# Mean squares with the squares as stationary operand, and GpSimd's first block sums held back behind the start

## The chip, the cores and the metric

The kernel runs on one core of one Trainium2 chip. The metric is the device time in microseconds of one execution; lower is better. TensorE multiplies, VectorE and ScalarE work on tiles, GpSimd does the same with its own program, and SyncE (SP) only issues transfers. Every engine runs its own instructions in the order in which they stand in its queue, and waits at an instruction until what it needs is done.

## The reference

One layer of a decoder trunk on 1024 rows of 1024 values, in float32. The part that the change touches, shortened:

```python
h = layer_norm(x, ln_in_g, ln_in_b)
proj = h @ w_in                       # 11,296 columns: 44 pairs of 256 and the dt columns
u, b_gate, c_gate, z_a, z_s, xbc, dt_raw, g_a, g_s = jnp.split(proj, ...)
y_a = (silu(z_a) * b_gate * conv3(c_gate * u)) @ w_a_out
y_s = ssd_chunked(...) + d_skip * xs  # scan over 8 chunks of 128 rows, 4 groups
hg = (y_s * silu(z_s)) in 4 groups of 512 channels
hg = hg * rsqrt(mean(square(hg)) + 1e-5)   # per row and group
y_s = (hg * norm_s_g) @ w_s_out
h = layer_norm(alpha * h + (sigmoid(g_a) * y_a + sigmoid(g_s) * y_s) @ w_o, ln_g, ln_b)
```

## The kernel before

**Start.** Eight tiles x0 to x7 of 128 rows are loaded by SP. `stats` and `factors` make mean and reciprocal deviation on VectorE with a root on ScalarE (L348), `norm` applies them (L362 on ScalarE, L360 on VectorE for x3 and x7). TensorE transposes the tiles by 128 x 128 blocks into eight PSUM banks: x0 to x3 at L397, x4 to x7 in `second_half` at L419. For each k, `evac` copies a bank to `hf` on ScalarE (L371), and VectorE makes from it a rounded high part (the cast L375) and a low part (`sub_split`, L106): `b11` and `b21` for the first half of the rows. Before that TensorE runs matmuls on a zeroed tile `warm` (L320).

**Products.** A pair is two weight tiles of 128 columns each. The pair's 256 columns times 1024 rows are computed as seven products of blocks (half of the depth by half of the rows) instead of eight (j = 1 to 7): 1 is a11 with b11, 2 is a12 with b21, 3 is s4 with b22, 4 is a22 with t4, 5 to 7 are s1 to s3 with t1 to t3. GpSimd makes s1, s2, s3 in `combine` (L239 to L245) and s4 in `combine_last` (L253); t1 to t4 come from `quarter_sums` on VectorE with copies by ScalarE (L434). Each weight block is split too: `whip` (high, ScalarE L279 or VectorE L281) and `wlop` (low, VectorE L106). A product is four times three matmuls with 512 moving columns: high by high (L979), high by low (L980), low by high (L981). The first three pairs (`EARLY` = 3) are computed while the second half of the rows is being normalised; their results go through `oa` (L995, L988). `dps` (L446, L447) is the projection for dt.

**Scan.** The 32 chunks (four groups of eight) run as small stages between the products of the other pairs. A chunk ends with squares on ScalarE, two folding additions on GpSimd (L705, L706) and `s_sum`: a matmul with one column of ones as the stationary operand and the folded squares as the moving one, the sum of 128 rows in one row of PSUM (L715), ScalarE's copy of that row (L717) and its store to the DRAM line `ssq_d` (L718). At the eighth chunk `group_rstd` reads the line back as 128 x 8 on GpSimd's queue (L724), takes the root (`rsqrt`: ScalarE L89, VectorE L90 to L97) and stores the factors to `rst_d` (L727) on the same queue. Later stages read them from there for the y products (L822 to L824).

**Order.** The list `items` sets the order of the products. For the early pairs it is products 1 and 2 of pair 0, of pair 1, of pair 2, then 3, 6, 5, 7, 4 of the three in turn. The scheduler merges this with the other work, and each engine keeps the order that results. SP issues the loads in program order: x0 to x3, the constants, the dt weights, the four blocks of pair 0, then the rest.

Of the kernel before, what the change touches and what calls it, by code (L numbers as in the profile page):

```python
# [19 lines left out]
F32 = mybir.dt.float32  # L20
F32R = mybir.dt.float32r
AF = mybir.ActivationFunctionType
ALU = mybir.AluOpType
PSUM = bass.MemoryType.PSUM

P = 128
L = 1024
D = 1024
KT = D // P
HALF = 512  # L30
NCH = 8
H = 32
G = 4
# [12 lines left out]
def trunk_kernel(ctx: ExitStack, tc: tile.TileContext, x, w_in, w_dt, w_a, w_s, w_o, par, con,  # L46
# [10 lines left out]
    bc_d = [tc.dram_tile([P, 2, L], F32, name=f"bc_d{g}") for g in range(G)]  # L57
    cum_d = tc.dram_tile([H, L], F32, name="cum_d")
    ecum_d = tc.dram_tile([H, L], F32, name="ecum_d")
    ssq_d = [tc.dram_tile([1, L], F32, name=f"ssq_d{g}") for g in range(G)]  # L60
    rst_d = [tc.dram_tile([1, L], F32, name=f"rst_d{g}") for g in range(G)]

    cst = ctx.enter_context(tc.tile_pool(name="cst", bufs=1))
# [21 lines left out]
    def rsqrt(pool, r, v, n, tag):  # L85

        ve = pool.tile([P, n], F32, tag=tag + "a", name=tag + "a")
        q = pool.tile([P, n], F32, tag=tag + "b", name=tag + "b")
        S.activation(q, v, AF.Sqrt, bias=eps_t, scale=1.0)  # L89
        V.tensor_scalar(ve, v, EPS, -0.5, ALU.add, ALU.mult)  # L90
        V.reciprocal(r, q)
        if n == 1:
            V.scalar_tensor_tensor(q, r, ve, r, ALU.mult, ALU.mult)
        else:
            V.tensor_tensor(q, r, r, ALU.mult)
            V.tensor_tensor(q, q, ve, ALU.mult)
        V.scalar_tensor_tensor(r, q, 1.5, r, ALU.add, ALU.mult)  # L97
# [7 lines left out]
    def sub_split(lo, full, hi, eng):  # L105
        return eng.tensor_tensor(lo, full, hi.bitcast(F32), ALU.subtract)  # L106
# [48 lines left out]
    def rawt(name):  # L155
        return ap.tile([P, HALF], F32, tag="raw", name=name, bufs=8)

    def bank(tag, name):
        return pa.tile([P, HALF], F32, tag=tag, name=name, bufs={"U": 2, "yy": 2}.get(tag, 1))
# [26 lines left out]
    EARLY = 3  # L186
# [6 lines left out]
    pairs += [gates[1], *conv_pairs[6], gates[2], gates[3], *conv_pairs[7], gates[4], gates[5], gates[6], gates[7]]  # L193
    NP = len(pairs)
    assert NP == 44
    items = [("p", p, j) for p in range(EARLY) for j in (1, 2)]
    items += [("p", p, j) for j in (3, 6, 5, 7, 4) for p in range(EARLY)]
    late = None
    for p in range(EARLY, NP):
        items += [("p", p, 1)] + ([late] if late else []) + [("p", p, j) for j in (2, 6, 5, 7, 4)]  # L200
# [9 lines left out]

    raws, s1s, ops = {}, {}, {}

    def fetch(n):

        if n >= len(items) or items[n][:2] in raws or items[n] in raws:
            return
        kind, i, j = items[n]
        if kind == "p":
            blocks = {}
            for w in ("a11", "a12", "a21", "a22"):  # L220
                k0 = (int(w[2]) - 1) * HALF
                r = est.tile([P, HALF], F32, name=f"e{i}_{w}") if i < 2 else rawt(f"raw{i}_{w}")
                SP.dma_start(r, w_in[pairs[i][int(w[1])], :, k0:k0 + HALF])
                blocks[w] = r
            raws[kind, i] = blocks
        else:
            r = rawt(f"raw_{kind}{i}_{j}")
            SP.dma_start(r, w_a[i, :, j * HALF:(j + 1) * HALF] if kind == "a" else
                         w_s[4 * i + j // 2, :, j % 2 * HALF:(j % 2 + 1) * HALF])
            raws[items[n]] = r  # L230

    def combine(p):

        if p in s1s:
            return
        r = raws["p", p]
        s1, s2 = (est.tile([P, HALF], F32, name=f"e{n}_{p}") if p < 2 and n == "s1" else
                  r["a11"] if p < 2 else ap.tile([P, HALF], F32, tag=n, name=f"{n}_{p}") for n in ("s1", "s2"))
        Gp.tensor_tensor(s1, r["a21"], r["a22"], ALU.add)  # L239
        if p < 2:  # L240
            Gp.tensor_tensor(r["a21"], r["a11"], r["a21"], ALU.subtract)
            Gp.tensor_tensor(s2, s1, r["a11"], ALU.subtract)
        else:
            Gp.tensor_tensor(s2, s1, r["a11"], ALU.subtract)
            Gp.tensor_tensor(r["a21"], r["a11"], r["a21"], ALU.subtract)  # L245
        s1s[p] = {"s1": s1, "s3": r["a21"], "s2": s2}
# [48 lines left out]


    xs = []
    for s in range(NCH):
        xt = full_unit(s, f"x{s}")
        SP.dma_start(xt, x[s * P:(s + 1) * P, :])  # L300
        xs.append(xt)
        if s == 3:
            SP.dma_start(con_t, con)
            SP.dma_start(par_t, par)
            wdt_raw = rawt("wdt_raw")[:, :KT * H].rearrange("p (k h) -> p k h", k=KT)
            SP.dma_start(wdt_raw, w_dt)
            fetch(0)

    db_t, al_t = (cdec_t.rearrange("p h c -> p (h c)")[:, i * H:(i + 1) * H] for i in range(2))
    SP.dma_start(db_t, dt_bias.partition_broadcast(P))  # L310
# [1 line left out]
    wdt = est.tile([P, KT, 2 * H], F32R, name="wdt")  # L312


    warm = rawt("warm")
    dT = [rawt("dT0"), rawt("dT1")]
    V.memset(warm, 0.0)
    wps = bank("c4", "warm")
    for i in range(7):
        PE.matmul(wps, lhsT=warm[:, :P], rhs=warm, start=True, stop=True)  # L320

    last = {}
# [1 line left out]
    def q(eng, f):  # L324

        if eng in last:
            with tc.issue_after(last[eng].ins):
                ins = f()
        else:
            ins = f()  # L330
        last[eng] = ins
        return ins
# [24 lines left out]
    def norm(s, eng):  # L357
# [3 lines left out]
        else:  # L361
            q(S, lambda: S.activation(xt, xt, AF.Identity, bias=nb, scale=r))  # L362


    hf = [{}, {}]

    def evac(hf_i, k, ps):
        if k % 4 not in hf[hf_i]:
            hf[hf_i][k % 4] = full_unit(8 + 2 * (k % 4) + hf_i, f"hf{hf_i}{k % 4}")
        full = hf[hf_i][k % 4][:, k // 4 * HALF:(k // 4 + 1) * HALF]  # L370
        q(S, lambda: S.activation(full, ps, AF.Identity, bias=pc(C_LB + k), scale=pc(C_LG + k)))  # L371
        name = {(0, 0): "b11", (0, 1): "b21", (1, 1): "b22"}.get((hf_i, k // 4))
        if name:
            u = b_unit(name, k % 4)
            q(V, lambda: V.tensor_copy(u[:, 0, :], full))  # L375
            q(V, lambda: sub_split(u[:, 1, :], full, u[:, 0, :], V))

    for s in (0, 1):
        stats(s, 0)
# [14 lines left out]
        last[V] = prep(0, V)  # L394
    for s in (0, 1, 3, 2):
        for k in range(KT):
            PE.transpose(trs[k][:, s % 4 * P:(s % 4 + 1) * P], xs[s][:, k * P:(k + 1) * P], ident)  # L397
    for k in range(KT):
        evac(0, k, trs[k])
        if k in (4, 6):  # L400
# [168 lines left out]
    later, now = {}, [0]  # L569
# [5 lines left out]
    def srows(g, c):  # L575
        return slice(c * P, (c + 1) * P)
# [131 lines left out]
    def s_store(n):  # L708
        g, c = divmod(n, NCH)
        SP.dma_start(gat_d[g][:, :, srows(g, c)], YT[n])  # L710

    def s_sum(n):
        g, c = divmod(n, NCH)
        ps = bank("tr", f"trs{n}")
        PE.matmul(ps[0:1, 256:384], lhsT=ones[:, 0:1], rhs=ZS[n][:, 0, :], start=True, stop=True)  # L715
        row = sd["p"].tile([1, P], F32, tag="row", name=f"row{n}", bufs=1)
        S.activation(row, ps[0:1, 256:384], AF.Copy, scale=1.0 / 512.0)  # L717
        S.dma_start(ssq_d[g][:, srows(g, c)], row)  # L718
        if c == NCH - 1:
            group_rstd(g)  # L720

    def group_rstd(g):
        ms = cst.tile([P, NCH], F32, tag="ms", name=f"ms{g}")
        Gp.dma_start(ms, ssq_d[g].squeeze(0).rearrange("(p c) -> p c", c=NCH))  # L724
        r = cst.tile([P, NCH], F32, tag="rr", name=f"rr{g}")
        rsqrt(cst, r, ms, NCH, "rq")
        Gp.dma_start(rst_d[g].squeeze(0).rearrange("(p c) -> p c", c=NCH), r)  # L727

    NS = G * NCH
    micro = []  # L730
# [492 lines left out]
```

## Time and profile before

| | |
|---|---|
| median of 3 runs | 1432.3 us (1431.84 to 1434.41) |
| profiled execution | 1434.14 us, its span 1432.2 us |
| TensorE | busy 1391.3 us, 97%, mean granted clock 0.991 |
| VectorE, ScalarE, GpSimd | busy 975.1, 708.8, 484.7 us |
| granted clock of TensorE in 20:25, 25:30, 30:35 us | 0.85, 0.50, 0.62; 1.00 in the slices from 35 to 80 |

The profile is one execution. Busy time counts the instructions of an engine; a wait is idle time of an engine, put down to what released it. A granted clock of 1.00 is 2.4 GHz, one of 0.50 is 1.2 GHz. Times in the rows are from the start of the span.

### The profile page before, as it was taken

The page shows a single profiled execution, that of the slowest core. Times are in us where ns is not written, and L with a number is a line of the kernel's source. Part 1 is how long each engine was busy: PE and PEld are TensorE (multiplying, and loading weights), DVE is VectorE, ACT ScalarE, POOL GpSimd, SP SyncE. Part 2 cuts the span into 40 slices and gives each one's busy share as a digit, 9 for nine tenths or more (in the row PEclk, how much of TensorE's full clock was granted, in tenths as well). Part 3 has the DMA queues.
Part 4 walks back from the last instruction along what each step waited for, and adds up shares of the span by engine and source line. Part 5 has one row for each costly group of instructions (what it writes and reads, how often), then busy time and mean ns, then how long its engine had stood idle before and what let it go on. Part 6 is the DMA issues. An engine that isn't in the chain of part 4 may idle for free. (4 is left out here: it accounts for less than half of the span.)

```text
span 1432.2 us, 18457 instructions
## 1 busy us (share of the span) xinstructions
PE 1391.3 (97%) x6522; PEld 1100.9 (77%) x6522; DVE 975.1 (68%) x1423; ACT 708.8 (49%) x1227; POOL 484.7 (34%) x374
## 2 busy tenths in 40 slices
PE   6999999999999999999999999999989999999997
PEld 3777877787877787877787777878768888888786
DVE  7967878877678867778877768585464463224774
ACT  3664556555557565566555665656452231113421
POOL 4012324444334534334535234444230000000496
PEclk8999999999999999999999999999999999999999
DMA  6022354545344555445554445454547764223322
GB/s 234 16 96 89 110 141 132 144 148 146 125 132 135 137 155 149 135 114 156 130 167 117 151 126 143 145 147 129 184 150 268 233 226 137 90 81 119 123 101 77
DMA packets 166717, 198.14 MB, mean 138 GB/s; under 512 B 10944, under 2 KB 116320, under 8 KB 166624
## 3 DMA queue, kind: packets, MB, share of 16 engines
q1 hardware_dynamic: 158096, 167.12, 39.7%
q10 hardware_dynamic: 8272, 29.81, 5.3%
q8 instruction: 51, 0.84, 0.2%
q14 instruction: 42, 0.34, 0.1%
q0 software_dynamic: 256, 0.03, 0.0%
HBM read 146.29 MB, written 50.63 MB: 137 GB/s over the span
## 5 line engine op out<-in xcount | busy, mean ns | idle before, releaser
L106 DVE TENSOR_TENSOR wlop<-raw_a,whip 128x512 fp32r<-128x512 f32 x210 | 183.1, 872 | 171.3 <-ACT whip L279 66.7
L979 PE MATMUL p<-b,whip 128*128 128x512 f32 x352 | 144.0, 410 | 3.6 <-ACT a L781 3.4
L979 PE MATMUL pU<-t,whip 128*128 128x512 f32 x352 | 144.7, 413 | 1.7 <-ACT oa L1014 1.7
L279 ACT ACTIVATE whip<-raw_a 128x512 fp32r<-128x512 f32 x210 | 127.6, 622 | 36.9 <-issue 10.5
L979 PE MATMUL p<-t,whip 128*128 128x512 f32 x352 | 141.8, 403 | 1.7 <-DVE oa L988 1.7
L980 PE MATMUL p<-b,whip 128*128 128x512 f32 x352 | 140.3, 399 | 0.0
L981 PE MATMUL p<-b,wlop 128*128 128x512 f32 x352 | 140.2, 398 | 0.0
L981 PE MATMUL pU<-t,wlop 128*128 128x512 f32 x352 | 139.1, 396 | 1.0 <-DVE wlop L106 0.9
L981 PE MATMUL p<-t,wlop 128*128 128x512 f32 x352 | 139.2, 395 | 0.4 <-DVE wlop L106 0.4
L980 PE MATMUL pU<-t,whip 128*128 128x512 f32 x352 | 139.0, 395 | 0.0
L980 PE MATMUL p<-t,whip 128*128 128x512 f32 x352 | 138.9, 395 | 0.0
L647 POOL TENSOR_TENSOR xw<-xd,dte_t 128x256 f32<-128x256 f32 x56 | 46.9, 838 | 258.7 <-DVE xd L633 258.7
L904 POOL TENSOR_TENSOR res<-res,ag 128x1024 f32<-128x1024 f32 x8 | 19.6, 2455 | 276.4 <-ACT res L903 271.6
L823 PE MATMUL p_ws<-y,whis 128*128 128x512 f32 x256 | 100.9, 394 | 0.0
L822 PE MATMUL p_ws<-y,whis 128*128 128x512 f32 x256 | 100.8, 394 | 0.0
L824 PE MATMUL p_ws<-y,wlos 128*128 128x512 f32 x256 | 100.7, 393 | 0.0
L106 DVE TENSOR_TENSOR wlos<-raw_s,whis 128x512 fp32r<-128x512 f32 x32 | 22.1, 692 | 113.0 <-PE p_ws L824 89.3
L239 POOL TENSOR_TENSOR s<-raw_a,raw_a 128x512 f32<-128x512 f32 x42 | 69.7, 1660 | 85.4 <-DVE wlop L106 81.7
L253 POOL TENSOR_TENSOR raw_a<-raw_a,s 128x512 f32<-128x512 f32 x42 | 66.0, 1571 | 95.5 <-issue 87.3
L979 PEld LDWEIGHTS p<-b,whip 128*128 128x128 f32 x352 | 66.9, 190 | 26.5 <-issue 4.3
L106 DVE TENSOR_TENSOR wlop<-s,whip 128x512 fp32r<-128x512 f32 x84 | 80.1, 966 | 9.4 <-PE p L981 6.3
L613 ACT ACTIVATE em<-em,cum_t 128x128 f32<-128x128 f32 x256 | 81.3, 389 | 7.3 <-ACT ob L557 4.4
(219 smaller groups left out, 3340.8 us busy)
## 6 DMA issues: line engine op xcount, KB each, us to landing
raw_a<-in_w_in_dram SPq DMA_DIRECT2D x168, 256.0 KB
em<-cum_d SPq DMA_DIRECT2D x64, 256.0 KB
xg_d<-cv ACTq DMA_DIRECT2D x16, 512.0 KB
xT<-xg_d SPq DMA_DIRECT2D x32, 256.0 KB
z<-zs_d SPq DMA_DIRECT2D x32, 256.0 KB
gat_d<-y SPq DMA_DIRECT2D x32, 256.0 KB
gt<-gat_d SPq DMA_DIRECT2D x16, 512.0 KB
raw_s<-in_w_s_dram SPq DMA_DIRECT2D x32, 256.0 KB
```

The lines of the kernel that those rows point to most:

```text
L106: return eng.tensor_tensor(lo, full, hi.bitcast(F32), ALU.subtract)
L239: Gp.tensor_tensor(s1, r["a21"], r["a22"], ALU.add)
L253: Gp.tensor_tensor(a12, a12, s1s[p]["s2"], ALU.subtract)
L279: S.activation(flat(hi), src, AF.Copy)
L613: S.activation(em[:, h, :], em[:, h, :], AF.Relu, bias=cum_t[:, 8 * g + 4 * i + h, c:c + 1], scale=-1.0)
L647: Gp.tensor_tensor(xw, XD[n, i], dte_t[:, hs, c].unsqueeze(2).to_broadcast([P, HG, HD]), ALU.mult)
L822: PE.matmul(ps, lhsT=hi[:, k, :], rhs=u[:, 0, :], start=start, stop=False)
L823: PE.matmul(ps, lhsT=hi[:, k, :], rhs=u[:, 1, :], start=False, stop=False)
L824: PE.matmul(ps, lhsT=lo[:, k, :], rhs=u[:, 0, :], start=False, stop=stop)
L979: PE.matmul(ps, lhsT=hi[:, k, :], rhs=u[:, 0, :], start=first, stop=False, skip_group_check=True)
L980: PE.matmul(ps, lhsT=hi[:, k, :], rhs=u[:, 1, :], start=False, stop=False, skip_group_check=True)
L981: PE.matmul(ps, lhsT=lo[:, k, :], rhs=u[:, 0, :], start=False, stop=(k == 3), skip_group_check=True)
```

## The change

- `warm` is zeroed by GpSimd, not VectorE, as its first work; six matmuls run on it instead of seven, and four more of 256 columns between the transposes of x1 and x3.
- SP's loads stand in another order: `a11` and `a12` of the three early pairs, the dt weights and x4 to x7 come ahead of all `a21` and `a22`. The dt weights go into the tile `dT0`.
- `items` has product 1 of the three early pairs, then product 2 of the three.
- In `combine`, the first sum of an early pair waits for `b_done[0]`, the last low split of `b21` (k = 3).
- `s_sum` has the folded squares as the stationary operand and the column of ones as the moving one. The sum of a chunk is a column of PSUM, which ScalarE copies into column c of the tile `MS[g]` in SBUF. `ssq_d`, the stores to it and the read are gone, `group_rstd` is merged into `s_sum`, and the store of the factors writes element (p, c) to position 128 c + p instead of 8 p + c.

```diff
@@ -57,7 +57,6 @@
     bc_d = [tc.dram_tile([P, 2, L], F32, name=f"bc_d{g}") for g in range(G)]
     cum_d = tc.dram_tile([H, L], F32, name="cum_d")
     ecum_d = tc.dram_tile([H, L], F32, name="ecum_d")
-    ssq_d = [tc.dram_tile([1, L], F32, name=f"ssq_d{g}") for g in range(G)]
     rst_d = [tc.dram_tile([1, L], F32, name=f"rst_d{g}") for g in range(G)]
 
     cst = ctx.enter_context(tc.tile_pool(name="cst", bufs=1))
@@ -193,8 +192,7 @@
     pairs += [gates[1], *conv_pairs[6], gates[2], gates[3], *conv_pairs[7], gates[4], gates[5], gates[6], gates[7]]
     NP = len(pairs)
     assert NP == 44
-    items = [("p", p, j) for p in range(EARLY) for j in (1, 2)]
-    items += [("p", p, j) for j in (3, 6, 5, 7, 4) for p in range(EARLY)]
+    items = [("p", p, j) for j in (1, 2, 3, 6, 5, 7, 4) for p in range(EARLY)]
     late = None
     for p in range(EARLY, NP):
         items += [("p", p, 1)] + ([late] if late else []) + [("p", p, j) for j in (2, 6, 5, 7, 4)]
@@ -210,19 +208,20 @@
 
     raws, s1s, ops = {}, {}, {}
 
+    def fetch_block(i, w):
+        blocks = raws.setdefault(("p", i), {})
+        k0 = (int(w[2]) - 1) * HALF
+        blocks[w] = est.tile([P, HALF], F32, name=f"e{i}_{w}") if i < 2 else rawt(f"raw{i}_{w}")
+        SP.dma_start(blocks[w], w_in[pairs[i][int(w[1])], :, k0:k0 + HALF])
+
     def fetch(n):
 
         if n >= len(items) or items[n][:2] in raws or items[n] in raws:
             return
         kind, i, j = items[n]
         if kind == "p":
-            blocks = {}
             for w in ("a11", "a12", "a21", "a22"):
-                k0 = (int(w[2]) - 1) * HALF
-                r = est.tile([P, HALF], F32, name=f"e{i}_{w}") if i < 2 else rawt(f"raw{i}_{w}")
-                SP.dma_start(r, w_in[pairs[i][int(w[1])], :, k0:k0 + HALF])
-                blocks[w] = r
-            raws[kind, i] = blocks
+                fetch_block(i, w)
         else:
             r = rawt(f"raw_{kind}{i}_{j}")
             SP.dma_start(r, w_a[i, :, j * HALF:(j + 1) * HALF] if kind == "a" else
@@ -236,7 +235,10 @@
         r = raws["p", p]
         s1, s2 = (est.tile([P, HALF], F32, name=f"e{n}_{p}") if p < 2 and n == "s1" else
                   r["a11"] if p < 2 else ap.tile([P, HALF], F32, tag=n, name=f"{n}_{p}") for n in ("s1", "s2"))
-        Gp.tensor_tensor(s1, r["a21"], r["a22"], ALU.add)
+        ins = Gp.tensor_tensor(s1, r["a21"], r["a22"], ALU.add)
+        if p < EARLY:
+            tc.add_manual_dep(ins.ins, b_done[0].name,
+                              mybir.DependencyInfo(mybir.DependencyClass.Sync, mybir.DependencyReason.DATA), reason="later")
         if p < 2:
             Gp.tensor_tensor(r["a21"], r["a11"], r["a21"], ALU.subtract)
             Gp.tensor_tensor(s2, s1, r["a11"], ALU.subtract)
@@ -295,16 +297,31 @@
 
 
     xs = []
-    for s in range(NCH):
+    dT = [rawt("dT0"), rawt("dT1")]
+    warm = rawt("warm")
+    Gp.memset(warm, 0.0)
+
+    def load_rows(s):
         xt = full_unit(s, f"x{s}")
         SP.dma_start(xt, x[s * P:(s + 1) * P, :])
         xs.append(xt)
-        if s == 3:
-            SP.dma_start(con_t, con)
-            SP.dma_start(par_t, par)
-            wdt_raw = rawt("wdt_raw")[:, :KT * H].rearrange("p (k h) -> p k h", k=KT)
-            SP.dma_start(wdt_raw, w_dt)
-            fetch(0)
+
+    for s in range(4):
+        load_rows(s)
+    SP.dma_start(con_t, con)
+    fetch_block(0, "a11")
+    SP.dma_start(par_t, par)
+    for i in (1, 2):
+        fetch_block(i, "a11")
+    for i in range(EARLY):
+        fetch_block(i, "a12")
+    wdt_raw = dT[0][:, :KT * H].rearrange("p (k h) -> p k h", k=KT)
+    SP.dma_start(wdt_raw, w_dt)
+    for s in range(4, NCH):
+        load_rows(s)
+    for i in range(EARLY):
+        for w in ("a21", "a22"):
+            fetch_block(i, w)
 
     db_t, al_t = (cdec_t.rearrange("p h c -> p (h c)")[:, i * H:(i + 1) * H] for i in range(2))
     SP.dma_start(db_t, dt_bias.partition_broadcast(P))
@@ -312,11 +329,8 @@
     wdt = est.tile([P, KT, 2 * H], F32R, name="wdt")
 
 
-    warm = rawt("warm")
-    dT = [rawt("dT0"), rawt("dT1")]
-    V.memset(warm, 0.0)
     wps = bank("c4", "warm")
-    for i in range(7):
+    for i in range(6):
         PE.matmul(wps, lhsT=warm[:, :P], rhs=warm, start=True, stop=True)
 
     last = {}
@@ -361,6 +375,8 @@
         else:
             q(S, lambda: S.activation(xt, xt, AF.Identity, bias=nb, scale=r))
 
+    b_done = [None]
+
 
     hf = [{}, {}]
 
@@ -373,7 +389,7 @@
         if name:
             u = b_unit(name, k % 4)
             q(V, lambda: V.tensor_copy(u[:, 0, :], full))
-            q(V, lambda: sub_split(u[:, 1, :], full, u[:, 0, :], V))
+            b_done[0] = q(V, lambda: sub_split(u[:, 1, :], full, u[:, 0, :], V)).ins
 
     for s in (0, 1):
         stats(s, 0)
@@ -394,7 +410,9 @@
         last[V] = prep(0, V)
     for s in (0, 1, 3, 2):
         for k in range(KT):
-            PE.transpose(trs[k][:, s % 4 * P:(s % 4 + 1) * P], xs[s][:, k * P:(k + 1) * P], ident)
+            q(PE, lambda: PE.transpose(trs[k][:, s % 4 * P:(s % 4 + 1) * P], xs[s][:, k * P:(k + 1) * P], ident))
+        for i in range(4 if s == 1 else 0):
+            q(PE, lambda: PE.matmul(trs[7][:, 256:HALF], lhsT=warm[:, :P], rhs=warm[:, :256], start=True, stop=True))
     for k in range(KT):
         evac(0, k, trs[k])
         if k in (4, 6):
@@ -709,22 +727,20 @@
         g, c = divmod(n, NCH)
         SP.dma_start(gat_d[g][:, :, srows(g, c)], YT[n])
 
+    MS = {}
+
     def s_sum(n):
+
         g, c = divmod(n, NCH)
+        if c == 0:
+            MS[g] = cst.tile([P, NCH], F32, tag="ms", name=f"ms{g}")
         ps = bank("tr", f"trs{n}")
-        PE.matmul(ps[0:1, 256:384], lhsT=ones[:, 0:1], rhs=ZS[n][:, 0, :], start=True, stop=True)
-        row = sd["p"].tile([1, P], F32, tag="row", name=f"row{n}", bufs=1)
-        S.activation(row, ps[0:1, 256:384], AF.Copy, scale=1.0 / 512.0)
-        S.dma_start(ssq_d[g][:, srows(g, c)], row)
+        PE.matmul(ps[:, 256:257], lhsT=ZS[n][:, 0, :], rhs=ones[:, 0:1], start=True, stop=True)
+        S.activation(MS[g][:, c:c + 1], ps[:, 256:257], AF.Copy, scale=1.0 / 512.0)
         if c == NCH - 1:
-            group_rstd(g)
-
-    def group_rstd(g):
-        ms = cst.tile([P, NCH], F32, tag="ms", name=f"ms{g}")
-        Gp.dma_start(ms, ssq_d[g].squeeze(0).rearrange("(p c) -> p c", c=NCH))
-        r = cst.tile([P, NCH], F32, tag="rr", name=f"rr{g}")
-        rsqrt(cst, r, ms, NCH, "rq")
-        Gp.dma_start(rst_d[g].squeeze(0).rearrange("(p c) -> p c", c=NCH), r)
+            r = cst.tile([P, NCH], F32, tag="rr", name=f"rr{g}")
+            rsqrt(cst, r, MS[g], NCH, "rq")
+            Gp.dma_start(rst_d[g].squeeze(0).rearrange("(c p) -> p c", p=P), r)
 
     NS = G * NCH
     micro = []
```

**GpSimd at the start.** These are GpSimd's rows from the dt weights on, before. A name is a tile with the number of its pair (`es1_0`, `s1_2` are s1 of pairs 0 and 2; `e0_a12` is a block of pair 0, and holds s4 behind L253).

```order
L391 CAST wdt_171<-wdt_raw_151 128x8x32
L392 ISA
L392 TENSOR_TENSOR wdt_171<-wdt_raw_151,wdt_171 128x8x32
L239 TENSOR_TENSOR es1_0_422<-e0_a21_157,e0_a22_159 128x512
L241 TENSOR_TENSOR e0_a21_157<-e0_a11_153,e0_a21_157 128x512
L242 TENSOR_TENSOR e0_a11_153<-es1_0_422,e0_a11_153 128x512
L253 TENSOR_TENSOR e0_a12_155<-e0_a12_155,e0_a11_153 128x512
L239 TENSOR_TENSOR es1_1_445<-e1_a21_346,e1_a22_348 128x512
L241 TENSOR_TENSOR e1_a21_346<-e1_a11_342,e1_a21_346 128x512
L239 TENSOR_TENSOR s1_2_469<-raw2_a21_354,raw2_a22_356 128x512
L244 TENSOR_TENSOR s2_2_470<-s1_2_469,raw2_a11_350 128x512
L242 TENSOR_TENSOR e1_a11_342<-es1_1_445,e1_a11_342 128x512
L245 TENSOR_TENSOR raw2_a21_354<-raw2_a11_350,raw2_a21_354 128x512
L253 TENSOR_TENSOR e1_a12_344<-e1_a12_344,e1_a11_342 128x512
```

And in the changed kernel, from the fill of `warm` on:

```order
L302 MEMSET warm_139 128x512
L407 CAST wdt_186<-dT0_137 128x8x32
L408 ISA
L408 TENSOR_TENSOR wdt_186<-dT0_137,wdt_186 128x8x32
L238 TENSOR_TENSOR es1_0_421<-e0_a21_172,e0_a22_174 128x512
L238 TENSOR_TENSOR es1_1_444<-e1_a21_176,e1_a22_178 128x512
L243 TENSOR_TENSOR e0_a21_172<-e0_a11_150,e0_a21_172 128x512
L243 TENSOR_TENSOR e1_a21_176<-e1_a11_153,e1_a21_176 128x512
L244 TENSOR_TENSOR e0_a11_150<-es1_0_421,e0_a11_150 128x512
L244 TENSOR_TENSOR e1_a11_153<-es1_1_444,e1_a11_153 128x512
L255 TENSOR_TENSOR e0_a12_157<-e0_a12_157,e0_a11_150 128x512
L255 TENSOR_TENSOR e1_a12_159<-e1_a12_159,e1_a11_153 128x512
```

The twelve sums of the three pairs are the same; the first sums of pairs 0 and 1 now stand side by side at the head of the row, both behind the hold, and those of pair 2 follow the s4 of pair 1 (behind the last row shown).

**ScalarE ahead of the second half.** Its rows from the conversion of pair 0's s4 (`whip0_3`) to the norm of x6, before:

```order
L279 ACTIVATE whip0_3_427<-e0_a12_155 128x512
L348 ACTIVATE ln1_4_313<-mv_t_122,eps_t_120 128x2
L279 ACTIVATE whip1_3_450<-e1_a12_344 128x512
L279 ACTIVATE whip2_3_475<-raw2_a12_352 128x512
L995 ACTIVATE oa2_453<-pU2_452 128x512
L362 ACTIVATE x4_161<-x4_161,nb_t_124,rs_t_123 128x1024
L362 ACTIVATE x5_163<-x5_163,nb_t_124,rs_t_123 128x1024
L279 ACTIVATE whip0_6_575<-e0_a11_153 128x512
L348 ACTIVATE ln1_6_332<-mv_t_122,eps_t_120 128x2
L362 ACTIVATE x6_165<-x6_165,nb_t_124,rs_t_123 128x1024
```

And in the changed kernel:

```order
L1011 ACTIVATE oa2_405<-pU2_404 128x512
L362 ACTIVATE ln1_4_327<-mv_t_118,eps_t_116 128x2
L281 ACTIVATE whip0_3_426<-e0_a12_157 128x512
L376 ACTIVATE x4_164<-x4_164,nb_t_120,rs_t_119 128x1024
L376 ACTIVATE x5_166<-x5_166,nb_t_120,rs_t_119 128x1024
L281 ACTIVATE whip1_3_449<-e1_a12_159 128x512
L281 ACTIVATE whip2_3_473<-raw2_a12_161 128x512
L362 ACTIVATE ln1_6_346<-mv_t_118,eps_t_116 128x2
L281 ACTIVATE whip0_6_573<-e0_a11_150 128x512
L376 ACTIVATE x6_168<-x6_168,nb_t_120,rs_t_119 128x1024
```

The copy of pair 2's first product (`oa2`) and the norms of x4 and x5 stand ahead of `whip1_3` and `whip2_3` now; both of these stand ahead of the root for x6 and x7 (`ln1_6`), as before.

**ScalarE at the end of the last group.** From the last product's weights to the root, before:

```order
L279 ACTIVATE whip43_5_9385<-s1_43_9320 128x512
L717 ACTIVATE row31_9403<-trs31_9401 1x128
L718 DMA ssq_d3_110<-row31_9403 1x128
L89 ACT_TABLE_LOAD
L89 ACTIVATE rqb_9410<-ms3_9406,eps_t_120 128x8
L279 ACTIVATE whip43_7_9440<-raw43_a21_9236 128x512
```

And in the changed kernel:

```order
L281 ACTIVATE whip43_5_9319<-s1_43_9254 128x512
L739 ACTIVATE ms3_7849<-trs31_9335 128x1
L88 ACT_TABLE_LOAD
L88 ACTIVATE rqb_9340<-ms3_7849,eps_t_116 128x8
L281 ACTIVATE whip43_7_9370<-raw43_a21_9170 128x512
```

The copy writes a column of 128 instead of a row, and no transfer stands between it and the root any more, on this queue or on GpSimd's.

## Rows read from the trace of the kernel before

**Rows 1.** Windows: span, busy us (count) PE PEld DVE ACT POOL, clock, DMA, GB/s.

```profile
25.00:30.00 5.00, 3.80 (x7) 2.08 (x8) 4.89 (x7) 1.49 (x3) 2.53 (x2) 0.50 0.00 1
...
70.00:75.00 5.00, 3.67 (x15) 2.15 (x14) 5.00 (x9) 1.89 (x3) 0.00 (x0) 1.00 0.00 0
```

**Rows 2.** Timeline of TensorE: start, us, line, operation, count, [idle before, its releaser].

```profile
17.07 3.66 PE L397 MATMUL tr<-con_t,x 128*128 128x128 f32 x32
...
52.58 3.33 PE L419 MATMUL tr<-con_t,x 128*128 128x128 f32 x20 [0.87 <-ACT hf L371]
...
55.92 0.50 PE L979 MATMUL p<-b,whip 128*128 128x512 f32 x1
```

**Rows 3.** Timeline of VectorE at the start.

```profile
13.91 1.11 DVE L355 SCALAR_TENSOR_TENSOR nb_t<-mv_t,rs_t 128x2 f32<-128x2 f32 x1
...
23.42 1.64 DVE L106 TENSOR_TENSOR b<-hf,b 128x512 fp32r<-128x512 f32 x1
...
28.08 0.41 DVE L375 CAST b<-hf 128x512 fp32r<-128x512 f32 x1
...
37.60 0.69 DVE L106 TENSOR_TENSOR b<-hf,b 128x512 fp32r<-128x512 f32 x1
```

**Rows 4.** Timeline of GpSimd at the start.

```profile
21.80 1.30 POOL L239 TENSOR_TENSOR es<-e_a,e_a 128x512 f32<-128x512 f32 x1 [1.77 <-DMA e_a<-in_w_in_dram]
...
24.47 1.72 POOL L239 TENSOR_TENSOR s<-raw_a,raw_a 128x512 f32<-128x512 f32 x1
```

**Rows 5.** Timeline of ScalarE before the second half's transposes.

```profile
47.81 0.28 ACT L348 ACTIVATE ln<-mv_t,eps_t 128x2 f32<-128x2 f32 x1
...
49.28 1.25 ACT L362 ACTIVATE x<-x,nb_t,rs_t 128x1024 f32<-128x1024 f32 x1 [1.19 <-DVE nb_t L355]
```

**Rows 6.** Waits: engine, line, releaser: us in total, times, longest.

```profile
DVE rqa L90 <- DMA ms<-ssq_d: 17.4, 4, 7.3
...
PE tr L621 <- DVE xd L633: 5.0, 4, 2.2
...
PE pU L979 <- ACT oa L1014: 1.7, 3, 0.7
```

**Rows 7.** Timelines of ScalarE, VectorE and TensorE at the last group's end.

```profile
1034.00 0.27 ACT L717 ACTIVATE row<-trs 1x128 f32<-1x128 f32 x1 [1.99 <-PE trs L715]
...
1034.57 1.28 ACT L89 ACT_TABLE_LOAD   x1 [0.30 <-ACT row L717]
...
1038.98 0.30 ACT L89 ACTIVATE rqb<-ms,eps_t 128x8 f32<-128x8 f32 x1 [3.12 <-DMA ms<-ssq_d]
...
1039.95 0.17 DVE L97 SCALAR_TENSOR_TENSOR rr<-rqb,rr 128x8 f32<-128x8 f32 x1
...
1041.46 0.47 PE L979 MATMUL p<-t,whip 128*128 128x512 f32 x1 [1.71 <-DVE oa L988]
...
1055.46 0.76 PE L979 MATMUL p<-b,whip 128*128 128x512 f32 x1 [3.41 <-ACT a L781]
...
1061.39 0.39 PE L824 MATMUL p_wa<-a,wloa 128*128 128x512 f32 x1
```

**Rows 8.** Timeline of TensorE: two stationaries of 128 columns, then two of one.

```profile
412.48 0.39 PE L626 MATMUL tr<-bc 128*128 128x128 f32 x2
...
412.62 0.48 PE L979 MATMUL p<-t,whip 128*128 128x512 f32 x1
...
421.42 0.38 PE L715 MATMUL trs<-z,con_t 128*1 128x128 f32 x2
...
421.73 0.51 PE L979 MATMUL p<-b,whip 128*128 128x512 f32 x1
```

**Rows 9.** Groups of TensorE's weight loads by form: count, busy us, mean ns.

```profile
L626 PEld LDWEIGHTS tr<-bc 128*128 128x128 f32 x64 | 9.7, 191 | 0.0
...
L715 PEld LDWEIGHTS trs<-z,con_t 128*1 128x1 f32 x64 | 2.7, 81 | 11.7 <-issue 5.5 <-POOL raw_a L253 4.4 <-POOL z L706 1.8
```

**Rows 10.** Timeline of GpSimd: one store of the group's factors.

```profile
428.08 0.55 POOL L727 DMA_DIRECT2D rst_d<-rr  x1 [2.69 <-DVE rr L97]
```

## The prediction, made before the changed kernel ran

> **What bounds the kernel now.** I read the page first: TensorE is busy 1391.3 of 1432.2 us, so 40.9 us are left that an edit elsewhere could give back, and what TensorE itself executes counts in full. The waits come next, to see where the idle time sits. Then I followed the timelines at the two places that the change touches: the first 60 us, and the ends of the four scan groups.
>
> At the start the chain runs load, statistics, transposes, ScalarE's evacuation, VectorE's high and low splits of `b11` and `b21`. In [rows 1] TensorE has 3.80 us of work in 25:30, at a granted clock of 0.50 (the 1.2 GHz level), while VectorE is busy 4.89 of 5: VectorE is the limit. Some of its instructions are slow only beside GpSimd's. A two-column operation takes 1.11 and a split 1.64, where a split in a stretch without GpSimd takes 0.69 and a cast 0.41 [rows 3]; GpSimd's sums lie under the slow ones [rows 4]. In 70:75 TensorE waits again, for t1 to t4: 3.67 busy of 5 [rows 1], so 1.33 us there can absorb a delay.
>
> At a group's end the mean squares go out to memory and back before the root: VectorE's first operation waits 17.4 us in four for that, 7.3 once [rows 6]. TensorE pays when VectorE's queue, blocked by this, is late: tr behind `xd` (5.0 in four) and pU behind `oa` (1.7 in three) [rows 6]; at the last group 1.71 and 3.41, then the low clock [rows 7].
>
> **The change part by part.**
>
> *Warm-up, load order.* The zero fill goes to GpSimd, whose first real work came later, so TensorE can begin earlier; six warm-up matmuls and four fillers lie in front of or between transposes that wait for the norms anyway. All loads but small ones were in by 25 us, when the DMA share is 0.00 [rows 1], and reordering changes none that the sum needs. I cost these at nothing. The cover is the wait for x2 and x3; without it four two-pass fillers of half a pass's columns would cost 1 to 2 us (a pass of 512 columns takes 0.235 to 0.43, below).
>
> *Held-back block sums.* The first sum of each early pair now waits for the last low split of `b21`; behind it on GpSimd stand all twelve sums. VectorE then runs free. Before, the last split ended at 37.60 + 0.69 = 38.3 [rows 3]. The two small slowed operations give back about 2 us and the fill on VectorE 0.5, so the transposes end near 16 (before 17.07 + 3.66 = 20.7 [rows 2], further split by waits). The first cast follows, then eight times 0.41 + 0.69 (8.8), two halves of statistics and three low splits (3.5 at 0.69): about 28.2. That is 10 us earlier. But only then do the sums begin, twelve in a row at 1.30 to 1.72 [rows 4]: 15.6 to 20.6, so they end at 44 to 49; I take 1.45, the lower half, since VectorE has less to do beside them: 45.6. What is late next: ScalarE's `whip2_3` needs the twelfth sum and stands ahead of the root for x6 and x7. From the conversion (about 0.6, like the row behind it), the root at 47.81 to the end of x6's norm at 49.28 + 1.25 is 2.7 [rows 5], and VectorE's share between is one low split more, 0.7. So x6 is ready near 49.6, against 50.5 before. TensorE's early products end near 38, so it idles some 10 us and starts the second transposes and the products behind them at the low clock. From x6 to the third product is 5.4 us (50.53 to 55.92 [rows 2, 5]), set by eight evacuations; it stays. Twelve matmuls at the low clock cost 12 x 0.2 = 2.4 (at the last group's end 14 lost 2.6, below), of which 1.33 is absorbed in 70:75. Result: -0.9 + 2.4 - 1.3, rounded up for the slower transposes: **+0.5**. Bounds: with sums at 1.30 and the idle time harmless, -2.5; at 1.72, +5.
>
> *Order of the early products* (1, 1, 1, 2, 2, 2). The same matmuls; only when `b11` or `b21` is needed changes. It is inside the term above: VectorE's end decides.
>
> *Squares as the stationary operand.* Each of 32 chunks had two passes with one stationary column and 128 moving; now 128 stationary columns and one moving. No row has the second form. From the first pass to the next product it took 421.73 - 421.42 = 0.31; two passes with 128 stationary columns took 412.62 - 412.48 = 0.14 [rows 8], though with 128 moving. That bound is -0.17 x 32 = -5.4. The other: a load of 128 columns takes 191 ns, one of one column 81 [rows 9]; bare, twice 0.11 more is +0.22 x 32 = +7.0. I lean to the row in context, as loads overlap products there, and take -0.10 x 32 = **-3.2**.
>
> The Trainium skill, "TensorE: Matmul & The Clock Gate", LDWEIGHTS (loading the stationary operand), speaks against this edit: a load costs by its number of stationary columns, 128 costing about 107 ns. The difference of the two rows agrees [rows 9]; by the rule alone the term would be an estimated +6.8 instead of -3.2.
>
> *Round trip gone.* ScalarE writes each chunk's mean squares into a column in SBUF; 32 stores by ScalarE and four reads by GpSimd vanish. At the last group ScalarE's copy is done at 1034.00 + 0.27, the table load takes 1.28 behind it [rows 7], so the root starts near 1035.6 instead of 1038.98 and the factors come 3.3 earlier than 1040.12. GpSimd also loses an issue, by the nearest row 0.55 [rows 10], so its sum comes 3.85 earlier. The payable waits: 5.0 less the longest 2.2, which lies at 209 us, ahead of the first group's end, leaves 2.8; pU behind `oa` 1.7; at the last group 1.71 and 3.41; then 14 matmuls from 1055.46 to 1061.39 take 5.93 where the fast pitch of 0.235 makes 3.3: 2.6. Sum 12.2. Not all goes: the restart at 1055.46 moves 3.85 earlier to 1051.6, while TensorE arrives at 1052.0 less 1.7, 0.5 and 0.7 of shorter waits, 49.1 past 1000; 2.5 of idling remains. The clock held behind the 2.2 of [rows 6] and fell behind 3.41 [rows 7]; I take 2.5 as still too short. **-9.7**. Bounds: -12.2, and -6.3 if 3.1 remains and the clock falls again.
>
> *Factors scattered.* The store of 128 x 8 factors becomes 1024 single elements instead of 128 pieces. An issue took 0.55 [rows 10]; bounds 0.55 and eight times that, 4.4. The larger one is what the factors' advance and the lost issue cover (3.3 + 0.55 + 0.55). Nothing; readers come much later.
>
> **Sum.** +0.5 - 3.2 - 9.7 = -12.4, from the profiled run's 1434.14 (span 1432.2 and 1.9 around it): 1421.7. That run is 1.8 above the median of the three runs timed, 1432.3, so **1419.9**.
>
> **Rivals.**
> 1. *GpSimd's chain costs the start more.* For it: the sums are now serial and ahead of x6's norm. At 1.72 each, 2 to 5 us lost: 1422 to 1425. A rule points the same way in its own manner: if transposes do not bring the clock up, the first products and those behind the second half's transposes run at 0.43 instead of 0.235 for longer, some 2 us: 1422. Against it: in [rows 1] products ran at the low level soon behind the first transposes; behind the second half's, the first product took 0.50 [rows 2], against 0.76 at the low level [rows 7]. The Trainium skill, "TensorE: Matmul & The Clock Gate", Part 4: PE-mode transpose, says that a transpose does not count as busy in the same way; the first of these observations agrees.
> 2. *Dear loads.* The second form costs 0 to +0.22 a chunk: 1423 to 1430, mostly about 1426.
> 3. *The start's 10 us survive in part*, if x6's norm comes before the sums' end matters: 1411 to 1414.
> 4. *The round trip was hidden anyway*: the waits return as VectorE waits for something else in the same place. For it: VectorE's queue is long. Gain 2 to 4 only: 1428 to 1430, the side of no change.
> 5. *Slower: the scattered store holds GpSimd.* Four stores of x us each; beyond the 4.4 that is covered all goes to the sums that products wait for. It cancels the gain of 12.4 at x = 4.4 + 3.1 = 7.5. At 20 us: +62 - 12 = about 1482. Against: eight times the pieces is 4.4 us.
>
> **How the numbers follow.** Forecast (1414 to 1422) 0.55; rival 1 0.17; rival 2 0.12; rival 3 0.07; rival 4 0.05; rival 5 0.04. The low bound is the start's -2.5 and squares' -5.4 with all 12.2 of the ends, 1412, less 1 for what is rounded: 1411; the high one holds rivals 1 and most of 2: 1428. What lies outside is rivals 4 and 5 and the edges of 2 and 3. A measurement of this kernel can tell about 0.2% (2.9 us) from no change. Faster 0.89; same 0.06 (rival 4 and the edge of 2); slower 0.05.
>
> **What would show it.** Last split of `b21` near 28; GpSimd's twelve sums back to back behind it, ending near 45.6; TensorE idle from about 38 to 49 and the clock down in that stretch; the third product near 55 to 56. At group ends no wait of `rqa` for a DMA; the factors 3.3 us earlier after the copy; tr behind `xd` and the idle 3.41 shrunk, no fall of the clock there. From the sum's first pass to the next product 0.2 instead of 0.31. The scattered store at most 4.4. It is wrong if the sums run slower than 1.72, if the form with 128 stationary columns takes over 0.31, or if the store is longer than 7.5.

## The result, and the profile after

The changed kernel takes 1419.5 us (median of 4 runs, 1419.38 to 1420.83), the kernel before 1432.5 beside it (1431.84 to 1434.41). The ratio is 0.9909, 95% interval 0.9892 to 0.9926. The profiled execution has a span of 1419.0 us. The forecast of 1419.9 is met, but not by its own terms.

From the third product on, TensorE runs the same instructions in the same order in both kernels. So the start of each can be subtracted from its partner's, and the difference followed through the program (worked out from the two timelines; positive is earlier in the changed kernel):

| stretch of the kernel before | gained there, us |
|---|---|
| up to the third product (55.92 before, 55.72 after) | 0.2 |
| the wait at 209 and the clock behind it | -0.8 |
| between the groups' ends: the sums | 8.3 |
| the first three groups' ends | 6.5 |
| the last group's end, up to the wait at 1055.46 | 3.4 |
| that wait, 3.41 before and 9.54 after | -6.1 |
| from there to the end: less time at the low clock behind waits | 1.7 |
| sum | 13.2 |

Two of these rows are not shown to be the change's. The wait at 209 is as long before and after (2.2), and only the clock behind it differs. Of the 1.7, 1.4 lie behind a wait of 1.8 us ahead of the `w_o` products that both kernels have too: the granted clock fell behind it before (0.72 in 1346:1352) and not after (1.00 in 1344:1352).

The windows of the changed kernel that answer to [rows 1] (columns as there), with the idle stretch between them:

```profile
25.00:30.00 5.00, 5.00 (x23) 3.99 (x22) 4.91 (x11) 1.03 (x2) 0.70 (x1) 1.00 0.00 2
40.00:45.00 5.00, 0.71 (x3) 0.29 (x3) 4.17 (x8) 1.54 (x2) 4.92 (x4) 0.71 0.05 12
45.00:50.00 5.00, 1.51 (x7) 1.52 (x8) 2.12 (x7) 3.06 (x5) 0.29 (x1) 0.50 0.26 93
50.00:55.00 5.00, 4.13 (x20) 3.73 (x19) 3.48 (x7) 4.17 (x6) 0.00 (x0) 0.50 0.00 0
70.00:75.00 5.00, 3.67 (x15) 2.17 (x15) 5.00 (x9) 1.89 (x3) 0.00 (x0) 1.00 0.00 0
```

In 25:30 TensorE is now full, at the high level. In 40:50 it has 2.2 of 10 us of work, and in 45:55 the clock is at the 1.2 GHz level. In 70:75 it waits as before. Its timeline and those of VectorE, GpSimd and ScalarE at the start, which answer to [rows 2 to 5]:

```profile
13.12 2.71 PE L415 MATMUL tr<-warm 128*128 128x256 f32 x8
...
48.48 2.18 PE L437 MATMUL tr<-con_t,x 128*128 128x128 f32 x9 [6.97 <-DVE x L374]
...
51.54 4.43 PE L437 MATMUL tr<-con_t,x 128*128 128x128 f32 x20 [0.87 <-ACT hf L387]
...
55.72 0.48 PE L995 MATMUL p<-b,whip 128*128 128x512 f32 x1
...
28.53 0.69 DVE L105 TENSOR_TENSOR b<-hf,b 128x512 fp32r<-128x512 f32 x1
...
29.30 2.54 POOL L238 TENSOR_TENSOR es<-e_a,e_a 128x512 f32<-128x512 f32 x2 [13.53 <-DVE b L105]
...
43.59 1.70 POOL L255 TENSOR_TENSOR raw_a<-raw_a,s 128x512 f32<-128x512 f32 x1
...
45.32 0.63 ACT L281 ACTIVATE whip<-raw_a 128x512 fp32r<-128x512 f32 x1 [3.78 <-POOL raw_a L255]
...
47.62 1.24 ACT L376 ACTIVATE x<-x,nb_t,rs_t 128x1024 f32<-128x1024 f32 x1 [0.96 <-DVE nb_t L369]
```

`b21`'s last low split ends at 29.2 instead of 38.3; then come GpSimd's twelve sums, from 29.30 to 45.3, 1.33 each; behind the last, `whip2_3` at 45.32 and x6's norm at 47.62. Twenty transposes of the second half take 4.43 us at the low clock, where before they took 3.33 at the high one [rows 2], and the third product starts only 0.2 us earlier than before. TensorE's waits (total, times, longest):

```profile
PE p L995 <- ACT a L797: 9.5, 1, 9.5
...
PE tr L437 <- DVE x L374: 7.0, 1, 7.0
...
PE tr L639 <- DVE xd L651: 2.2, 1, 2.2
```

The waits of [rows 6] for `xd` have gone except for the one at 209, and those of pU for `oa` are gone; the wait for `a` at the last group's end, 3.4 before, is 9.5. The last group's end, against [rows 7], with GpSimd's store, SP's first load of `w_a` and ScalarE's use of that load:

```profile
1019.88 0.17 ACT L739 ACTIVATE ms<-trs 128x1 f32<-128x1 f32 x1 [1.80 <-PE trs L738]
...
1021.36 0.30 ACT L88 ACTIVATE rqb<-ms,eps_t 128x8 f32<-128x8 f32 x1
...
1022.33 0.17 DVE L96 SCALAR_TENSOR_TENSOR rr<-rqb,rr 128x8 f32<-128x8 f32 x1
...
1022.79 0.92 POOL L743 DMA_DIRECT2D rst_d<-rr  x1 [8.45 <-DVE rr L96]
...
1025.38 0.39 PE L995 MATMUL p<-t,whip 128*128 128x512 f32 x1
...
1028.12 4.96 SPq L227 DMA_DIRECT2D raw_a<-in_w_a_dram  x1
...
1039.18 0.63 ACT L281 ACTIVATE whia<-raw_a 128x512 fp32r<-128x512 f32 x1 [7.75 <-DMA raw_a<-in_w_a_dram]
...
1043.97 0.77 PE L995 MATMUL p<-b,whip 128*128 128x512 f32 x1 [9.54 <-ACT a L797]
```

The mean squares are there at 1020.05, the factors at 1022.5, without a transfer. TensorE's 1.71 of idle time at 1041.46 is gone (1025.38 follows without a gap). But SP's first load of `w_a` takes 4.96 us to issue. ScalarE idles 7.75 us for it, and the pieces of `a` that TensorE needs stand behind that in ScalarE's queue, so TensorE stands still until 1043.97. The sum of a chunk, against [rows 8]; the product ahead of it stood before at

```profile
421.10 0.39 PE L981 MATMUL p<-b,wlop 128*128 128x512 f32 x1
```

and now the three are:

```profile
419.85 0.39 PE L997 MATMUL p<-b,wlop 128*128 128x512 f32 x1
420.08 0.28 PE L738 MATMUL trs<-con_t,z 128*128 128x1 f32 x2
420.22 0.47 PE L995 MATMUL p<-b,whip 128*128 128x512 f32 x1
```

From the first pass to the next product it is 0.14 instead of 0.31, and from the product ahead to the first pass 0.23, where before 0.32. Over 32 chunks the time between the neighbouring products falls from 20.2 to 12.2 us, that is by 8.0 (the table's 8.3 is all that is gained between the groups' ends).

### The profile page after: what moved, and what is told of

Its sections match the earlier page's. It is cut to its first block, busy times and chain, and to the rows that moved or that the text cites. A ratio compares the mean times of both kernels' runs of the same rounds, so it can differ in the third digit from the quotient of the medians.

```text
span 1419.0 us, 18392 instructions
## 1 busy us (share of the span) xinstructions
PE 1379.9 (97%) x6528; PEld 1112.4 (78%) x6528; DVE 973.2 (69%) x1422; ACT 704.3 (50%) x1227; POOL 486.2 (34%) x371
## 5 line engine op out<-in xcount | busy, mean ns | idle before, releaser
L281 ACT ACTIVATE whip<-raw_a 128x512 fp32r<-128x512 f32 x210 | 127.5, 622 | 26.6 <-issue 10.5
```

Source lines behind the costliest of these rows:

```text
L281: S.activation(flat(hi), src, AF.Copy)
```

## The experiments

After the result I held that the store of 1024 single elements stops the transfers that stand behind it, that the sums and the first groups' ends pay more than forecast, and that the start's gain is eaten by GpSimd's sums. The rivals are in the expectations. The kernel before was run beside each; ratios are to it.

**The factors stored in 128 pieces, as before.** (The factors then lie in another order than the readers take them; work and sizes are the same.)

```diff
-            Gp.dma_start(rst_d[g].squeeze(0).rearrange("(c p) -> p c", p=P), r)
+            Gp.dma_start(rst_d[g].squeeze(0).rearrange("(p c) -> p c", c=NCH), r)
```

> The changed kernel with one line altered: the factors of a group go out as 128 pieces of 8 elements, as before the change, instead of 1024 single elements; they land in another order than the readers expect, so y is scaled by wrong factors. Theory A (the store of single elements holds up the transfers behind it: ScalarE's store of the gate takes 1.14 us a packet and SP's first load of w_a 4.96 us to issue, so TensorE waits 9.5 us at the last group's end): the issue takes at most 1.1 us, the wait shrinks to 3.5 us or less, and the time falls by about 6 us, to 1412 to 1415 us. Theory B (TensorE merely arrives earlier at loads whose time is set by SP's queue and its other waits): the wait stays at 9 to 10 us, the time at 1419.5, within 1 us.

Measured: 1411.9 us, ratio 0.9851 (0.9835 to 0.9868), 7.6 us under the changed kernel. SP's issue and TensorE's wait in its timeline:

```profile
1025.71 0.43 SPq L227 DMA_DIRECT2D raw_a<-in_w_a_dram  x1
...
1035.71 0.47 PE L995 MATMUL p<-b,whip 128*128 128x512 f32 x1 [3.69 <-ACT a L797]
```

The issue takes 0.43, the wait 3.69. In the DMA issues around the last group's end (KB, median us to landing) ScalarE's store of the gate, issued just behind the factors, lands in 2.8 us here:

```profile
sgs_d<-oa ACTq DMA_DIRECT2D x1, 512.0 KB, 2.8
```

and in 10.5 in the changed kernel:

```profile
sgs_d<-oa ACTq DMA_DIRECT2D x1, 512.0 KB, 10.5
```

The changed kernel's windows around the store:

```profile
1024.00:1026.00 2.00, 2.00 (x10) 1.64 (x9) 0.14 (x1) 1.60 (x3) 1.04 (x1) 1.00 0.42 78
1026.00:1028.00 2.00, 2.00 (x11) 1.59 (x10) 2.00 (x2) 2.00 (x4) 1.30 (x1) 1.00 3.12 66
```

The packets' time comes to a DMA share of 3.12 in 1026:1028, while 66 GB/s move. The packets that begin there are 32 of ScalarE's store, of 4 KB each. GpSimd itself was held for 0.92 us only. Theory A holds, though the edges of its ranges are missed by a little (a wait of 3.69 against at most 3.5, and 1411.9 against 1412). Why ScalarE's packets take so long while the single elements go out, no run here shows. Followed through the trace of the changed kernel run again (below), whose third product starts within 0.2 us of this one's, 0.6 of the gain lies at the first two groups' ends and 7.0 at the last.

**Only the new sums**, on the start of before (the hunks on `ssq_d` and `s_sum` alone):

> The kernel before with the new sums alone (squares as the stationary operand, no round trip, store of single elements); the start is that of before. Theory A (the start of the changed kernel is worth nothing, as the alignment of the two traces says: +0.2 us at the third product): 1419.7 us, within 1.5. Theory B (the start pays several us that are lost again later): 1423 us or more.

Measured: 1421.9, ratio 0.9917 (0.9903 to 0.9932); and **only the start** (the same hunks undone):

> The changed kernel with the sums of before (one stationary column, stores to memory, read back, contiguous store of the factors); so the start alone is changed. Theory A: 1432.3 us, within 1.5, that is no change; last split of b21 near 29, GpSimd's twelve sums end near 45, TensorE idle some 9 us before the second half's transposes. Theory B: 1424 to 1429.

Measured: 1430.7, ratio 0.9980 (0.9971 to 0.9990). The first is just above theory A's range, the second just below. So the sums give 0.8% and the start, by what is left of the whole change and by its own run, 0.1 to 0.2% or 1 to 3 us. The start is not the same in each execution: in the profile of the changed kernel the fillers' stretch, 10:15, had a granted clock of 0.66, and eight fillers took 2.71; in that of the same kernel run again 1.00, and they took 1.89 (first the one's window, then the other's window and fillers):

```profile
10.00:15.00 5.00, 4.73 (x21) 4.16 (x22) 4.54 (x13) 3.98 (x7) 1.02 (x2) 0.66 1.04 395
```

```profile
10.00:15.00 5.00, 4.57 (x32) 4.08 (x33) 4.54 (x13) 3.98 (x7) 1.15 (x2) 1.00 1.06 399
```

```profile
12.45 1.89 PE L415 MATMUL tr<-warm 128*128 128x256 f32 x8
```

> The changed kernel itself once more, beside the others on one chip: 1419.5 us, within 1.5. In its profile the granted clock during the fillers behind the warm-up (10 to 15 us) is either 0.66, and the third product starts near 55.7, or 1.00, and it starts near 54.

Measured: 1419.9, ratio 0.9908 (0.9894 to 0.9921). With the clock at 1.00 the third product started at 54.11, 1.6 us earlier than in the other execution.

**Without the hold** (the added dependency in `combine` left out):

> The changed kernel without the hold: the first sums of the early pairs start when a21 and a22 have landed, at 20 to 25 us. Theory A (the hold moves the wait from VectorE to GpSimd's sums and is itself what costs): the sums end 3 to 6 us earlier, VectorE's splits of b21 some 3 us later, x6's norm 2 to 4 us earlier, the time 1415.5 to 1418 us. Theory B (free splits are worth more than early sums): 1420 to 1424 us.

Measured: 1420.7, ratio 0.9909 (0.9895 to 0.9924): the hold is worth nothing either way. GpSimd and VectorE:

```profile
20.33 1.53 POOL L238 TENSOR_TENSOR es<-e_a,e_a 128x512 f32<-128x512 f32 x1 [5.03 <-DMA e_a<-in_w_in_dram]
...
38.19 1.27 POOL L252 TENSOR_TENSOR raw_a<-raw_a,s 128x512 f32<-128x512 f32 x1
...
35.45 1.64 DVE L105 TENSOR_TENSOR b<-hf,b 128x512 fp32r<-128x512 f32 x1
...
43.32 0.69 DVE L1001 TENSOR_TENSOR oa<-p,oa 128x512 f32<-128x512 f32 x1 [2.38 <-PE p L994]
```

The sums end 6 us earlier, as A says, but the last split of `b21` 8 us later, where it says some 3, and VectorE then waits for TensorE's early products (43.32). x6's norm ends at 50.4, later and not earlier. The time lies inside theory B's range, but at its lower edge, and the ratio is that of the changed kernel: that free splits are worth more is not shown either.

**The last group's store, twice differently.** Turned by TensorE into 8 pieces of 512 bytes, or issued six products later:

```diff
+                pt = bank("tr", f"trr{g}")
+                PE.transpose(pt[:NCH, 256:384], r, ident)
+                t = cv(f"rt{g}")[:NCH, :P]
+                S.activation(t, pt[:NCH, 256:384], AF.Copy)
+                Gp.dma_start(rst_d[g].squeeze(0).rearrange("(c p) -> c p", p=P), t)
...
+                later.setdefault(now[0] + 6, []).append(out)
```

> The changed kernel with the last group's factors turned by TensorE (one 128 x 8 transpose, two products later) and stored as 8 pieces of 512 bytes; the other three groups keep the store of single elements. Theory A (the last group's store of single elements alone costs the stall): SP's first load of w_a takes about 0.43 us to issue as with the contiguous store, the wait at the last group's end is 3.5 to 4 us, the time 1411.5 to 1413.5 us. Theory B (the stores of the first three groups cost as well, or the turn is in the way): 1414 us or more.

> The changed kernel with the last group's store of single elements issued six products later, all else the same. Theory A (it is the place of the store, ahead of ScalarE's store of the gate and SP's loads of w_a, that costs): the wait at the last group's end 3.5 to 4 us, time 1412 to 1413.5 us. Theory B (the transfers that it now stands ahead of are needed as soon): 1415 to 1420 us, the wait found further on.

Measured: 1415.1, ratio 0.9870 (0.9854 to 0.9886), and 1414.3, 0.9869 (0.9846 to 0.9892). Both remove the stall (waits of 3.2 and 3.4 us). Both are above theory A's range. The profiles show where: the late store's third product came 1.8 us later than in the kernel with 128 pieces, with the fillers at 0.66 again, and the turned store's w_o products ran 2.8 us longer, at the low clock behind a wait of 1.81 that both have. Neither is the store's. But 0.6 us of either difference arise at the first two groups' ends, where both still store single elements; to that extent theory B of the first run is right.

**x6's norm ahead of the conversions of products 3**, alone and with the turned store:

> The changed kernel with the conversions of the three early pairs' s4 (products 3) placed behind x6's norm on ScalarE; nothing else in the program. Theory A (in the changed kernel x6's norm, and with it TensorE's idle time before the second half, waits for GpSimd's twelfth sum through ScalarE's and VectorE's order): x6's norm ends near 45 instead of 48.9, the third product starts 3 to 5 us earlier, the time is 2.5 to 5 us lower: 1414.5 to 1417 us. Theory B (VectorE's own work beside GpSimd's sums sets that time): less than 1 us, 1419 to 1420.

> Both at once: turned store of the last group's factors, and x6's norm ahead of the conversions. The two lie 1000 us apart and should add: Theory A 1407 to 1409.5 us; Theory B (gains at the start are lost again at the next wait) as the turned store alone, 1411.5 to 1413.5.

Measured: 1420.1, ratio 0.9904 (0.9887 to 0.9921), and 1412.9, 0.9857 (0.9841 to 0.9873). Both times are as theory B has them (1420.1 at the edge of its range). Alone it gives nothing that can be measured, and the 2.1 us under the turned store alone do not come from the start: in the profiles the products there run 0.6 us later. ScalarE and the third product:

```profile
43.31 1.24 ACT L379 ACTIVATE x<-x,nb_t,rs_t 128x1024 f32<-128x1024 f32 x1 [4.72 <-DVE nb_t L372]
44.45 1.14 ACT L282 ACTIVATE whip<-e_a 128x512 fp32r<-128x512 f32 x2
45.49 0.61 ACT L282 ACTIVATE whip<-raw_a 128x512 fp32r<-128x512 f32 x1
...
47.79 0.78 ACT L390 ACTIVATE hf<-tr,par_t 128x512 f32<-128x512 f32 x1 [0.69 <-PE tr L441]
...
52.80 0.78 PE L999 MATMUL p<-b,whip 128*128 128x512 f32 x1
```

The norm is ready at 44.6, as A says, but the conversions now stand between it and the evacuations, which begin at 47.79. Most of the wait had only moved: the third product starts 1.3 us ahead of that of the changed kernel run again, but at the low clock (0.78), and 0.4 of that is left a few products on.

**The order mended behind the norm too**, with the late store: the copy of dps ahead of x6's norm, pair 2's conversion on GpSimd, the low splits behind x7's norm.

```diff
+        if kind == "p" and i < EARLY and j == 3:
+            with tc.issue_after(x7_done):
+                return sub_split(flat(lo), source(n), flat(his[n]), V)
...
                 dt_project(0)
+                norm(6, S)
                 second_half()
```

> The changed kernel with the late store of the last group's factors, and at the start: x6's norm behind the copy of dps on ScalarE and no longer behind GpSimd's twelfth sum; pair 2's s4 is converted by GpSimd right behind that sum, and the low splits of the three s4 stand behind x7's norm on VectorE. The conversions that stood between x6's norm and the evacuations when the norm alone was moved are thus ahead of it or on GpSimd. Theory A (the 8 us of idle time before the second half come from the order on ScalarE and VectorE behind the sums): x6's norm ends near 44.5, the third product starts at 50 to 51.5 us, the time is 3 us below the late store alone, 1409 to 1412. Theory B (the idle time and the low clock behind it just move): the third product at 53 or later, 1413 to 1415.

Measured: 1409.8 (1408.92 to 1410.8), ratio 0.9835 (0.9822 to 0.9849): the fastest kernel here, 4.5 us under the late store alone. GpSimd, ScalarE and the third product:

```profile
43.15 0.63 POOL L283 CAST whip<-raw_a 128x512 fp32r<-128x512 f32 x1
...
43.83 1.24 ACT L379 ACTIVATE x<-x,nb_t,rs_t 128x1024 f32<-128x1024 f32 x1 [2.38 <-DVE nb_t L372]
46.70 1.45 ACT L390 ACTIVATE hf<-tr,par_t 128x512 f32<-128x512 f32 x2 [1.63 <-PE tr L440]
...
51.26 0.47 PE L1006 MATMUL p<-b,whip 128*128 128x512 f32 x1
```

The evacuations begin at 46.70 and the third product at 51.26. Theory A holds. But not all of the 4.5 us is the order's: the late store's profile had the fillers at 0.66 and this one at 1.00. Against the changed kernel run again, with the fillers at 1.00, the third product is 2.9 us earlier.

**The sum's matmul twice:**

> The changed kernel with the matmul of the sum issued a second time into the next PSUM column, which nothing reads: two more passes with 128 stationary columns and one moving column in each of the 32 chunks. Theory A (the new form costs about 0.14 us for two passes, as two passes with 128 stationary columns did beside it before): 0.12 to 0.18 us more a chunk, 4 to 6 us more in all, 1423.5 to 1425.5. Theory B (loads of 128 columns cost in full, twice 0.19): 12 us more, 1431.

Measured: 1427.0, ratio 0.9955 (0.9941 to 0.9969), 7.1 above the changed kernel:

```profile
421.75 0.40 PE L998 MATMUL p<-b,wlop 128*128 128x512 f32 x1
421.99 0.50 PE L739 MATMUL trs<-con_t,z 128*128 128x1 f32 x4
422.35 0.48 PE L996 MATMUL p<-b,whip 128*128 128x512 f32 x1
```

Two more passes cost 0.22, or 0.11 a pass, between the theories, where the two passes of the changed kernel together take 0.14. The loads in the changed kernel's trace show why: the first pass's begins with the product ahead (419.85) and runs beside it, and the second pass starts only 0.03 behind the first; the second's load begins with the first pass, and the next product starts 0.11 behind the second pass.

## Why the prediction came out right

- *Start, +0.5 forecast, -0.2 in the profile.* The order of events came as forecast: the last split at 29.2 (28.2 forecast), twelve sums until 45.3 (45.6), idle from about 39.5, x6's norm at 48.9 (49.6), the low clock in the idle stretch. The prices behind x6's norm were wrong. The 5.4 from there to the third product did not stay: they became 6.9, with the transposes themselves at the low clock. The twelve matmuls at the low clock, +2.4, did not come: the products from 55.72 on ran at the high level, and the lead of 0.2 us is the same at 200. So nothing was absorbed in 70:75 either. That the term came near is luck. Over several executions the start is worth 1 to 3 us by the two part kernels; a part of the spread is the clock in the fillers, which I had not priced.
- *Squares as stationary operand, -3.2 forecast, -8.0 measured.* Mis-sized. The bound from the row in context (-0.17) was exact for what lies behind the first pass; that the gap ahead of the first pass would shrink too (0.09), I had not counted. The Trainium skill, "TensorE: Matmul & The Clock Gate", LDWEIGHTS (loading the stationary operand), has about 107 ns for a load of 128 columns. The trace agrees where short passes follow each other (the sum twice: 0.11 a pass), but the estimate of +6.8 worked out from it did not come, since beside a product two passes added only 0.14.
- *Groups' ends, -9.7 forecast.* Mis-sized by place. The first three gave 6.5, where I counted 4.5; the last should have given 5.2 and lost 2.7 (3.4 - 6.1). With the store in 128 pieces the wait was 3.69, against the 2.5 forecast, and the clock fell behind it (0.66 in 1035:1040). The lower bound of this term, -6.3, comes to -6.5 from its own numbers.
- *The scattered store, nothing forecast.* This step failed. I priced it on GpSimd's queue (0.92 us, well under the 4.4), named no transfer of another queue behind it; rival 5 had the cause and missed the place. It costs 7.6 us through ScalarE's store and SP's loads.
- That 2.5 us of idling would not lower the clock, since 2.2 had not, rested on one execution: behind the same 2.19 at 209 the changed kernel's clock fell, and in the kernel before it held. The 2.5 itself never came.

The total was right by luck: two errors, 5 on the sums and 6 at the ends, cancel.

## What to carry to other kernels

Price a DMA by what stands behind it on all queues, not by its issuer: a store of single elements cost 0.9 us where it was issued and 7.6 us in other engines' transfers. When a wait goes, ask what stands next in the same queue: moving x6's norm alone gave nothing, mending what stood behind it too brought the third product 2.9 us forward, with the clock in the fillers alike. And follow paired instructions through two traces before a matching total is taken for a matching reason.

## What the hardware showed unexpectedly

The granted clock does not answer the same way to the same idle time. Behind the wait of 2.19 us near 208, which all profiled executions here share, products fell to the low level for a while in all but three (the kernel before, the start alone, the mended start). What decides it, no run shows. Nor does it answer the same way to the second half's transposes behind the long idle stretch: in the changed kernel's profile it stayed at 0.50 through all of them and rose with the third product; in that of the start alone it was 1.00 from 53 on, while transposes ran until 53.86. And while a store of 4 KB in single elements went out, 32 packets of ScalarE's store, 4 KB each, took times that come to a DMA share of 3.12, with 66 GB/s moved.
